# High weights over both halves of the activations in one 512-column matmul, halves added at read-out

## The chip, the cores and the metric

One core of a Trainium2 chip runs the whole layer. The time is device microseconds from start to end of one execution of that core's program; the median of several executions is compared.

## The reference

One layer of a hybrid backbone on 256 latent tokens and 256 context tokens of 4096 channels. Both are normed and modulated by an `adaLN` vector, then sent through one input projection of 13,312 columns, whose parts feed three mixers: a convolution module, a two-way gated linear recurrence and a neighbourhood attention that also reads the context. Each mixer's output is gated by a SiLU of its own part, all are concatenated, projected, added to the input and normed.

```python
hl = rmsnorm(xl, norm_g) * (1.0 + sc_l) + sh_l
hc = rmsnorm(xc, norm_g) * (1.0 + sc_c) + sh_c
a_val_l, a_glu_l, a_gate_l, r_x_l, r_gate_l, q_l, k_l, v_l, c_gate_l = split_proj(hl @ w_in)
... = split_proj(hc @ w_in)
...
mix_l = jnp.concatenate([ya_l * jax.nn.silu(a_gate_l), yb_l * jax.nn.silu(r_gate_l),
                         yc_l * jax.nn.silu(c_gate_l)], axis=-1)
xl_new = xl + g_l * (mix_l @ w_out)
```

All of it is in float32. The kernel makes each large float32 product out of three products of `float32r` operands: weights are split into a high part `hi` and a rest `lo`, activations likewise into part 0 and part 1, and it sums high x part 0, high x part 1 and low x part 0.

## The kernel before

The program is one long unrolled list in three phases. **Phase 1** (up to about 944 us of the trace) makes the modulation, the normed activations `LH` (latent) and `CH` (context), and those parts of the projection that both need (`r_x`, context keys, values) block by block over the contraction, with sums kept in pages `acc`. **Phase 2** (about 944 to 2004 us) makes the other parts of the projection for the latent tokens in chunks of 512 output columns over all 32 tiles of the contraction: values and gates of the convolution (`conv_in`), keys, queries and gates of four groups of four attention heads (`att_group`), and after these the gate of the recurrence, the pointwise product `w_pw` (8 tiles of contraction) and the gate of the convolution. **Phase 3** is the output projection (`gemm_tm`).

A chunk of phase 2 is one call of `gemm_cm` (L340): for each loaded pair of contraction tiles, four tiles of 128 output channels, and for each of these and each contraction tile `k` three matmuls of 256 moving columns (the 256 tokens): high weights on part 0, high weights on part 1, low weights on part 0, all into the same 256-column region of a bank. Each matmul has a weight load of its own. Two tiles of output channels share a bank of 512 columns, so a chunk takes two of the five banks of the tag "g" (L72). Phase 2 has 20 such chunks of 32 contraction tiles and 2 (`w_pw`) of 8.

`weights` (L327) loads 4 contraction tiles at a time as `raw` (1 MB on SP's queue, three buffers, shared with the loads of `w_ada` that `background` mixes in), ScalarE rounds two tiles to `hi` (L338), VectorE subtracts to get `lo` (L339); three buffers each. When a chunk ends its banks are read out by one instruction of 512 columns each, and the SiLU gates read the bank twice (L571, L572). Read-outs and the weight split stand under `hp()`, a high priority for the planner (`schedule_with_timeline_sim=True`), which fixes the order on each engine at build time. Convolutions, recurrences and the attention of heads go beside the products at lower priority; SBUF tiles come from one pool of `NPG` = 75 pages of 2 KB. GpSimd issues the attention's bias loads (L584).

In phase 1 the `r_x` chunks (`gemm_cm` with two moving operands) and the value chunks (`gemm_tm` with four stationary ones) each take four of the five banks "g"; they are emptied by `spill` (L499). Phase 3's `gemm_tm` uses matmuls of 512 columns, one weight load each.

Of the kernel before, what the change touches and what calls it, by code (L numbers as in the profile page):

```python
# [12 lines left out]
AF = mybir.ActivationFunctionType  # L13
# [11 lines left out]
    0, 1024, 2048, 3072, 4096, 5120, 7168, 9216, 11264)  # L25
# blocks of the contraction in the first phase, in tiles of 128
BLOCKS = [1, 2, 3, 3, 3, 4, 4, 4, 4, 4]
# from this block on, every second one's shift is summed on the vector engine
PAIRED = 8
# pages of 2 KB, buffers of weights as loaded and as split  # L30
NPG, NRAW, NHI = 75, 3, 3
# tiles of the contraction kept for the second half of the last chunk
HELD = 12
# urgency of what the tensor engine waits for
HP = 200000
# rates of the loads that go beside the products, by phase
ADA_A, ADA_B, CAP = 2.15, 1.2, 4.0
G1, G2, G3 = 0.4, 0.3, 0.4
# chunks of the last block that a recurrence follows; order of the second phase
REC1 = (1, 2, 4, 6, 8)  # L40
# [4 lines left out]
def tile_hybrid_layer(ctx: ExitStack, tc: tile.TileContext, x, c, cctx_tok, c_ctx, w_ada, b_ada,  # L45
# [13 lines left out]
    def background(weight):  # L59
        """emits queued units of loads between those of the products, at the set rate"""  # L60
        bg["credit"] = min(bg["credit"] + bg["rate"](weight), CAP)
        while bg["q"] and bg["credit"] >= 2.0:
            bg["credit"] -= 2.0
            bg["q"].pop(0)()
# [57 lines left out]

    # silu(c), silu(c_ctx) as channel columns, padded to 32 stationary columns
    scol = cp.tile([P, 64], F32, name="scol")
# [40 lines left out]
    def ada_units(k0, s, parts=(0, 1), on_vector=False):  # L165
# [92 lines left out]
    def rsqrt(y, v, t):  # L258
        """y = v ** -0.5, the table's root refined by a Newton step"""
        A.activation(y, v, AF.Sqrt)  # L260
        V.reciprocal(y, y)
        V.tensor_mul(t, y, y)
        V.tensor_mul(t, t, v)
        V.tensor_scalar(t, t, -0.5, 1.5, ALU.mult, ALU.add)
        V.tensor_mul(y, y, t)

# [1 line left out]
    ss = cp.tile([P, 4, 8], F32, name="ss")  # L268
# [56 lines left out]

# [1 line left out]
    def weights(view, ks, c0):  # L327
        """tiles of the weights, up to 4 loaded and 2 split at a time: [(tiles of the contraction, high, low)]"""
        for i in range(0, len(ks), 4):
# [12 lines left out]
    def gemm_cm(view, ks, c0, movs):  # L342
        """channel-major: out[n, t] for 4 tiles of n and each moving operand, 256 columns a region"""
        nb = 2 * len(movs)
# [14 lines left out]
        return banks  # L359

    def gemm_tm(view, ks, c0, stats, end=True):
        """token-major: out[t, n] for each stationary operand, 512 columns"""
        banks = [bank("g", "gtm") for _ in stats]
# [20 lines left out]
    def columns():  # L384
# [4 lines left out]
        V.tensor_scalar(hpw, col("b_pw", 0, 8), 0.5, None, ALU.mult)  # L389
        # 4 softplus(-lam), softplus(-lam) = (max(-lam, 0) + log1p(exp(-|lam|))), log1p(e) = 2 atanh(e / (2 + e))  # L390
        lm = col("lam", 0, 16)
# [21 lines left out]
    def ybs(n):  # L413
        """where the two directions' sum of head n lies: half a page of the inputs of a pair of heads"""
        return acc[("r", n // 4), n % 4 // 2 * 2][:, (n % 2) * T:(n % 2) * T + T]

    def recurrence(n):
# [22 lines left out]
        for d in range(2):  # L440
            xc, e, ti = rec[d]
            ci = cis[d]
            pr = bank("aux", "pr")
            nc.tensor.matmul(pr, gw[:, d, 0], xc, start=True, stop=True)
            pi = bank("aux", "pi")
            nc.tensor.matmul(pi, gw[:, d, 1], xc, start=True, stop=True)
            A.activation(ti, pi, AF.Tanh, bias=hbi[:, ci:ci + 1], scale=0.5)
            # 2 sigmoid(z) = exp(min(z, 0)) (1 + |tanh(z / 2)|)
            A.activation(e, pr, AF.Relu, bias=nbr[:, ci:ci + 1], scale=-1.0)
            A.activation(pr, pr, AF.Tanh, bias=hbr[:, ci:ci + 1], scale=0.5)  # L450
            prs.append(pr)
# [29 lines left out]

# [1 line left out]
    acc = {}  # L483
    side = [lambda n=n: recurrence(n) for n in range(8)]

    def aside(n=1):
        """emits the next pieces of work that need few products, among the chunks of those that need many"""
        for _ in range(n):
# [16 lines left out]
    while bi < len(BLOCKS):  # L505
        if bi < PAIRED:
            aq += ada_units(starts[bi], BLOCKS[bi])
        else:
            # the second block's shift is summed on the vector engine, spread among the other three parts
            pe = ada_units(starts[bi], BLOCKS[bi]) + [lambda bi=bi: done.add(bi)]  # L510
# [46 lines left out]

# [1 line left out]
    ALLK = list(range(KT))  # L559
# [6 lines left out]

    def silu2(b):
        """2 silu(b), a page"""
        t = page([P, 512], name="sil")
        with hp():  # L570
            A.activation(t, b, AF.Tanh, scale=0.5)  # L571
            V.scalar_tensor_tensor(t, t, 1.0, b, ALU.add, ALU.mult)  # L572
        return t

# [45 lines left out]

    # queries lie from right to left within a grid row, so that the bias rows are read with a stride of +1
    def att_group(g):
        kl, q, cg = [], [], []
        for b in gemm_cm(win, ALLK, C_K + 512 * g, [LH]):
            t = page([P, 2, T], name="kl")
            with hp():
                A.copy(t.rearrange("p a b -> p (a b)"), b)
            kl += [t[:, 0], t[:, 1]]
        aside()
        for b in gemm_cm(win, ALLK, C_Q + 512 * g, [LH]):  # L630
            t = page([P, 2, T], name="q")
            with hp():
                A.mul(t.rearrange("p a (r c) -> p (a r) c", c=64)[:, :, ::-1],
                      b.rearrange("p (r c) -> p r c", c=64), SCALE)
            q += [t[:, 0], t[:, 1]]
        aside()
        for b in gemm_cm(win, ALLK, C_CG + 512 * g, [LH]):
            t = silu2(b).rearrange("p (a b) -> p a b", a=2)
            cg += [t[:, 0], t[:, 1]]
# [6 lines left out]
    def conv_in(g):  # L646
        vals = []
        for b in gemm_cm(win, ALLK, C_VAL + 512 * g, [LH]):
            t = page([P, 512], name="val")
            with hp():  # L650
                A.mul(t, b, 0.5)
            vals.append(t)
        aside()
        for bi, b in enumerate(gemm_cm(win, ALLK, C_GLU + 512 * g, [LH])):
            t = page([P, 512], name="glu")
            with hp():
                A.activation(t, b, AF.Tanh, scale=0.5)
            for j in range(2):
# [59 lines left out]
    for g in range(2):  # L718
        for bi, b in enumerate(gemm_cm(win, ALLK, C_RG + 512 * g, [LH])):
            t = silu2(b)  # L720
            for j in range(2):
# [5 lines left out]
    for g in range(2):  # L727
        for bi, b in enumerate(gemm_cm(wpw, list(range(8)), 512 * g, [SH])):
            t = page([P, 512], name="pw")
            for j in range(2):  # L730
                n = 4 * g + 2 * bi + j
                with hp():
                    V.tensor_scalar(t[:, j * T:j * T + T], b[:, j * T:j * T + T], 0.25, hpw[:, n:n + 1],
                                    ALU.mult, ALU.add)
            PW.append(t)
    for g in range(2):
        for bi, b in enumerate(gemm_cm(win, ALLK, C_AG + 512 * g, [LH])):
            t = silu2(b)
            pw = PW[2 * g + bi]
# [3 lines left out]

# [1 line left out]
    korder = list(range(16, 32)) + list(range(8, 16)) + list(range(8))  # L745
# [3 lines left out]
    for oc in range(8):  # L749
# [27 lines left out]
        if oc < 7:  # L777
# [4 lines left out]
            continue  # L782
        # last chunk: the second token tile comes behind the first by HELD tiles of the contraction
        gate()
# [37 lines left out]
def _window():  # L822
    """neighbourhood mask by shape alone: rows are (query row parity, query column from the right),
    columns are key columns; a factor and an addend"""
    qc = 63 - np.arange(P) % 64
# [27 lines left out]
```

## Time and profile before

| | us |
|---|---|
| median of 3 executions | 2377.08 |
| lowest and highest | 2374.56, 2380.82 |
| span of the profiled execution | 2371.5 |
| TensorE busy with matmuls in it | 2315.1 (98%) |
| weight loads busy in it | 2034.4 (86%) |
| VectorE busy | 1580.3 (67%) |
| ScalarE busy | 945.7 (40%) |

The profiled execution is told by its span, from the first to the last instruction; the three timed executions lie 3 to 9 us above it. TensorE's two records of a product are read together: "PE" is the matmul, "PEld" the load of its stationary operand, which goes on while the matmul before it runs. A matmul's recorded duration overlaps the next one's, so its price is the distance from its start to the next start.

### The profile page before, as it was taken

The page shows a single profiled execution, that of the slowest core. Times are in us where ns is not written, and L with a number is a line of the kernel's source. Part 1 is how long each engine was busy: PE and PEld are TensorE (multiplying, and loading weights), DVE is VectorE, ACT ScalarE, POOL GpSimd, SP SyncE. Part 2 cuts the span into 40 slices and gives each one's busy share as a digit, 9 for nine tenths or more (in the row PEclk, how much of TensorE's full clock was granted, in tenths as well). Part 3 has the DMA queues.
Part 4 walks back from the last instruction along what each step waited for, and adds up shares of the span by engine and source line. Part 5 has one row for each costly group of instructions (what it writes and reads, how often), then busy time and mean ns, then how long its engine had stood idle before and what let it go on. Part 6 is the DMA issues. An engine that isn't in the chain of part 4 may idle for free.

```text
span 2371.5 us, 38433 instructions
## 1 busy us (share of the span) xinstructions
PE 2315.1 (98%) x16013; PEld 2034.4 (86%) x16013; DVE 1580.3 (67%) x2289; ACT 945.7 (40%) x1228; POOL 95.8 (4%) x150
## 2 busy tenths in 40 slices
PE   6899999999999999999999999999999999999997
PEld 4667777777788998999999899999999999888886
DVE  4465545445778779987879596955766666665555
ACT  5322212222223246886433343344444434434444
POOL 0000000000000001000000101101001001000000
PEclk9999999999999999999999999999999999999999
DMA  9888788877877544656776767767576678775664
GB/s 312 270 279 272 254 298 298 295 266 252 295 269 258 192 163 174 222 183 213 245 233 203 188 215 202 204 215 188 182 245 171 207 265 301 264 263 187 191 192 173
DMA packets 293461, 551.27 MB, mean 232 GB/s; under 512 B 10959, under 2 KB 52647, under 8 KB 293287
## 3 DMA queue, kind: packets, MB, share of 16 engines
q1 hardware_dynamic: 287856, 536.91, 66.1%
q0 software_dynamic: 4480, 11.54, 4.3%
q8 instruction: 125, 2.05, 0.3%
q10 hardware_dynamic: 951, 0.37, 0.1%
q14 instruction: 49, 0.40, 0.0%
HBM read 544.58 MB, written 4.19 MB: 231 GB/s over the span
## 4 chain that ended last, share of the span: by engine, by line
PE 83%; DMA 8%; DVE 4%; ACT 3%; issue 1%; SPq 0%; DVEq 0%; ACTq 0%
PE gcm L355 48%; PE gtm L371 9%; PE gtm L372 8%; PE gtm L370 8%; PE psa L217 5%; DMA raw<-in_w_ada_dram 4%; DMA raw<-in_w_in_dram 3%; DVE lo L339 2%; PE y L614 1%; ACT hi L338 1%; DMA xp<-in_ctx_dram 1%; DVE gacc L245 1%; PE pt L607 1%; PE sc L593 0%; PE sc L594 0%
## 5 line engine op out<-in xcount | busy, mean ns | idle before, releaser
L339 DVE TENSOR_TENSOR lo<-raw,hi 128x1024 fp32r<-128x1024 f32 (+1 forms) x630 | 747.4, 1189 | 556.8 <-ACT hi L338 552.9
L338 ACT CAST hi<-raw 128x1024 fp32r<-128x1024 f32 (+1 forms) x630 | 640.1, 1022 | 1171.9 <-PE gcm L355 492.8
L355 PE MATMUL gcm<-lh,hi 128*128 128x256 f32 x5632 | 1069.5, 285 | 2.9 <-ACT hi L338 2.8
L355 PEld LDWEIGHTS gcm<-lh,hi 128*128 128x128 f32 x5632 | 896.8, 192 | 18.3 <-issue 13.4
L355 PE MATMUL gcm<-lh,lo 128*128 128x256 f32 x2816 | 796.2, 285 | 4.2 <-DVE lo L339 4.0
L355 PEld LDWEIGHTS gcm<-lh,lo 128*128 128x128 f32 x2816 | 537.8, 192 | 11.6 <-DVE lo L339 5.8
L355 PE MATMUL gcm<-ch,hi 128*128 128x256 f32 x1536 | 326.6, 287 | 3.4 <-ACT hi L338 2.3
L355 PEld LDWEIGHTS gcm<-ch,hi 128*128 128x128 f32 x1536 | 259.0, 191 | 36.3 <-issue 27.8
L245 DVE SCALAR_TENSOR_TENSOR gacc<-raw,scol,gacc 128x512 f32<-128x512 f32 x248 | 185.8, 749 | 49.6 <-DMA raw<-in_w_ada_dram 47.1
L355 PE MATMUL gcm<-ch,lo 128*128 128x256 f32 x768 | 217.6, 286 | 0.0
L371 PE MATMUL gtm<-lo,mix 128*128 128x512 f32 x488 | 192.0, 393 | 0.1
L372 PE MATMUL gtm<-hi,mix 128*128 128x512 f32 x488 | 190.1, 390 | 0.0
L370 PE MATMUL gtm<-hi,mix 128*128 128x512 f32 x488 | 171.1, 390 | 0.0
L355 PEld LDWEIGHTS gcm<-ch,lo 128*128 128x128 f32 x768 | 146.5, 191 | 12.8 <-issue 9.0
L217 PE MATMUL psa<-raw,cpad 128*32 128x512 f32 (+3 forms) x1216 | 132.5, 521 | 7.9 <-DMA raw<-in_w_ada_dram 7.8
L499 DVE TENSOR_TENSOR acc<-acc,gcm 128x512 f32<-128x512 f32 x144 | 96.1, 682 | 37.7 <-PE gcm L355 37.1
L371 PEld LDWEIGHTS gtm<-lo,mix 128*128 128x128 f32 x488 | 91.6, 188 | 20.5 <-DVE lo L339 1.3
L370 PEld LDWEIGHTS gtm<-hi,mix 128*128 128x128 f32 x488 | 91.5, 188 | 19.2
L499 DVE TENSOR_TENSOR acc<-acc,gtm 128x512 f32<-128x512 f32 x144 | 94.3, 680 | 19.9 <-PE gtm L372 19.7
L372 PEld LDWEIGHTS gtm<-hi,mix 128*128 128x128 f32 x488 | 91.7, 188 | 18.4
L673 DVE SCALAR_TENSOR_TENSOR cv<-upad,cols,cv 128x256 f32<-128x256 f32 x240 | 105.6, 483 | 0.0
L371 PE MATMUL gtm<-lo,ch 128*128 128x512 f32 x256 | 102.2, 399 | 0.2 <-DVE lo L339 0.2
(218 smaller groups left out, 2107.9 us busy)
## 6 DMA issues: line engine op xcount, KB each, us to landing
raw<-in_w_in_dram SPq DMA_DIRECT2D x210, 1024.0 KB, 5.2
raw<-in_w_ada_dram SPq DMA_DIRECT2D x156, 1024.0 KB, 5.5
raw<-in_w_out_dram SPq DMA_DIRECT2D x61, 1024.0 KB, 5.5
raw<-in_w_ada_dram SPq DMA_DIRECT2D x48, 768.0 KB, 5.9
raw<-in_w_in_dram SPq DMA_DIRECT2D x30, 768.0 KB, 6.1
raw<-in_w_in_dram SPq DMA_DIRECT2D x10, 512.0 KB, 5.4
xp<-in_ctx_dram SPq DMA_DIRECT2D x16, 256.0 KB, 5.8
xp<-in_x_dram SPq DMA_DIRECT2D x16, 256.0 KB, 5.4
```

What stands on the lines that cost most here:

```text
L217: nc.tensor.matmul(st["ps"][32 * q:32 * q + 32, :W], cpad[k // 16][:, k % 16, :], raw[:, j, :], start=(k < 4), stop=(k >= KT - 4))
L245: V.scalar_tensor_tensor(st["a"], raw[:, j], s, st["a"], ALU.mult, ALU.add)
L338: A.copy(hi[:, :n], raw[:, o:o + n])
L339: V.tensor_sub(lo[:, :n], raw[:, o:o + n], hi[:, :n].bitcast(F32))
L355: nc.tensor.matmul(banks[r // 2][:, (r % 2) * T:(r % 2) * T + T], w[:, j, nt * P:(nt + 1) * P], movs[m][k][:, part], start=first, stop=las ...
L370: nc.tensor.matmul(banks[b], hh, wh[:, j], start=first, stop=False)
L371: nc.tensor.matmul(banks[b], hh, wl[:, j], start=False, stop=False)
L372: nc.tensor.matmul(banks[b], hl, wh[:, j], start=False, stop=last)
L499: V.tensor_add(acc[key, i], acc[key, i], b)
L607: nc.tensor.transpose(ps[:, kt * T + qt * P:kt * T + qt * P + P], Ps[qt][:, (2 * kp + kt) * P:(2 * kp + kt + 1) * P], ident)
L614: nc.tensor.matmul(ps[:, :T], acc[("v", h // 4), kt][:, i * P:(i + 1) * P], Ps[kt // 2][:, (kt % 2) * T:(kt % 2) * T + T], start=(kt == 0) ...
L673: V.scalar_tensor_tensor(o, upad[n][:, tap:tap + T], cw(tap, n), o, ALU.mult, ALU.add)
```

## The change

In phase 2 `gemm_cm` is replaced by `gemm_hl`: the high weights are loaded once and run over both parts of the activations as one matmul of 512 columns into a whole bank (left half the product with part 0, right half that with part 1); the low weights follow on part 0 into the left half. So two matmuls and two weight loads stand where three of each stood, and a chunk takes four banks. `joined` adds the halves at read-out: ScalarE copies the right half of each bank into a page, VectorE adds the left half to it. What follows (`tanh`, the reversed query copy, the SiLU product) then reads pages, at ordinary priority. The pool grows to 81 pages; the scratch for GpSimd's DMA descriptors is set to 4096. `gemm_cm` and `gemm_tm` stay in phases 1 and 3.

```diff
-NPG, NRAW, NHI = 75, 3, 3
+NPG, NRAW, NHI = 81, 3, 3
...
+    def gemm_hl(view, ks, c0, mov):
+
+        banks = [bank("g", "ghl") for _ in range(4)]
+        for kp, wh, wl in weights(view, ks, c0):
+            for nt in range(4):
+                for j, k in enumerate(kp):
+                    sl = slice(nt * P, (nt + 1) * P)
+                    nc.tensor.matmul(banks[nt], wh[:, j, sl], mov[k].rearrange("p a t -> p (a t)"),
+                                     start=k == ks[0], stop=False, skip_group_check=True)
+                    nc.tensor.matmul(banks[nt][:, :T], wl[:, j, sl], mov[k][:, 0],
+                                     start=False, stop=k == ks[-1], skip_group_check=True)
+            background(1)
+        return banks
+
+    def joined(banks, name, scale=None, bias=None):
+
+        for i in range(0, 4, 2):
+            u, t = page([P, 2, T], name="half"), page([P, 2, T], name=name)
+            with hp():
+                for j in range(2):
+                    b = banks[i + j]
+                    if bias is not None:
+                        A.activation(u[:, j], b[:, T:], AF.Identity, bias=bias[:, i + j:i + j + 1], scale=scale)
+                    elif scale is not None:
+                        A.mul(u[:, j], b[:, T:], scale)
+                    else:
+                        A.copy(u[:, j], b[:, T:])
+                    if scale is not None:
+                        V.scalar_tensor_tensor(t[:, j], b[:, :T], scale, u[:, j], ALU.mult, ALU.add)
+                    else:
+                        V.tensor_add(t[:, j], b[:, :T], u[:, j])
+            yield t, u
...
-    def silu2(b):
-        """2 silu(b), a page"""
-        t = page([P, 512], name="sil")
-        with hp():
-            A.activation(t, b, AF.Tanh, scale=0.5)
-            V.scalar_tensor_tensor(t, t, 1.0, b, ALU.add, ALU.mult)
-        return t
+    def silu2(zu):
+
+        z, u = zu
+        A.activation(u, z, AF.Tanh, scale=0.5)
+        V.scalar_tensor_tensor(u.rearrange("p a b -> p (a b)"), u.rearrange("p a b -> p (a b)"), 1.0,
+                               z.rearrange("p a b -> p (a b)"), ALU.add, ALU.mult)
+        return u.rearrange("p a b -> p (a b)")
...
-        for b in gemm_cm(win, ALLK, C_K + 512 * g, [LH]):
-            t = page([P, 2, T], name="kl")
-            with hp():
-                A.copy(t.rearrange("p a b -> p (a b)"), b)
+        for t, _ in joined(gemm_hl(win, ALLK, C_K + 512 * g, LH), "kl"):
...
-        for b in gemm_cm(win, ALLK, C_Q + 512 * g, [LH]):
-            t = page([P, 2, T], name="q")
-            with hp():
-                A.mul(t.rearrange("p a (r c) -> p (a r) c", c=64)[:, :, ::-1],
-                      b.rearrange("p (r c) -> p r c", c=64), SCALE)
+        for z, t in joined(gemm_hl(win, ALLK, C_Q + 512 * g, LH), "z", SCALE):
+            A.copy(t.rearrange("p a (r c) -> p (a r) c", c=64)[:, :, ::-1],
+                   z.rearrange("p a (r c) -> p (a r) c", c=64))
...
-        for b in gemm_cm(win, ALLK, C_VAL + 512 * g, [LH]):
-            t = page([P, 512], name="val")
-            with hp():
-                A.mul(t, b, 0.5)
-            vals.append(t)
+        for t, _ in joined(gemm_hl(win, ALLK, C_VAL + 512 * g, LH), "val", 0.5):
+            vals.append(t.rearrange("p a b -> p (a b)"))
...
-                with hp():
-                    V.tensor_scalar(t[:, j * T:j * T + T], b[:, j * T:j * T + T], 0.25, hpw[:, n:n + 1],
-                                    ALU.mult, ALU.add)
-            PW.append(t)
+        for t, _ in joined(gemm_hl(wpw, list(range(8)), 512 * g, SH), "pw", 0.25, hpw[:, 4 * g:4 * g + 4]):
+            PW.append(t.rearrange("p a b -> p (a b)"))
...
-    nc = _bacc.Bacc("TRN2", target_bir_lowering=False, num_devices=1)
+    nc = _bacc.Bacc("TRN2", target_bir_lowering=False, num_devices=1, dynamic_dma_scratch_size=4096)
```

The gates of attention, recurrence and convolution and the convolution's second input change in the same way as the queries: `gemm_hl`, `joined` into a page `z`, then `tanh` and product on pages.

## Rows read from the trace of the kernel before

**Rows 1.** The page's head: span, and TensorE's busy time and share

```profile
span 2371.5 us, 38433 instructions
PE 2315.1 (98%) x16013; PEld 2034.4 (86%) x16013; DVE 1580.3 (67%) x2289; ACT 945.7 (40%) x1228; POOL 95.8 (4%) x150
```

**Rows 2.** The chain that ended last: shares of the span by line

```profile
PE gcm L355 48%; PE gtm L371 9%; PE gtm L372 8%; PE gtm L370 8%; PE psa L217 5%; DMA raw<-in_w_ada_dram 4%; DMA raw<-in_w_in_dram 3%; DVE lo L339 2%; PE y L614 1%; ACT hi L338 1%; DMA xp<-in_ctx_dram 1%; DVE gacc L245 1%; PE pt L607 1%; PE sc L593 0%; PE sc L594 0%
```

**Rows 3.** Busy time by stretch; last: granted clock, DMA share, GB/s

```profile
944.00:2003.60 1059.60, 1047.32 (x8351) 1026.58 (x8351) 784.76 (x1122) 513.11 (x644) 79.66 (x113) 1.00 0.68 214
944.00:990.00 46.00, 45.78 (x356) 43.27 (x356) 42.87 (x55) 41.07 (x52) 2.72 (x5) 1.00 0.59 202
1140.00:1160.00 20.00, 20.00 (x169) 20.00 (x168) 18.63 (x31) 9.49 (x11) 0.00 (x0) 1.00 0.63 213
1320.00:1340.00 20.00, 15.66 (x116) 14.92 (x115) 11.71 (x18) 7.46 (x11) 3.30 (x4) 0.90 0.68 167
2280.00:2320.00 40.00, 40.00 (x178) 33.12 (x177) 20.88 (x21) 17.54 (x20) 0.00 (x0) 1.00 0.64 204
```

**Rows 4.** Groups by line and form: latent matmuls of `gemm_cm`, count first

```profile
L355 PE MATMUL gcm<-lh,hi 128*128 128x256 f32 x5632 | 1069.5, 285 | 2.9 <-ACT hi L338 2.8
L355 PE MATMUL gcm<-lh,lo 128*128 128x256 f32 x2816 | 796.2, 285 | 4.2 <-DVE lo L339 4.0
L355 PE MATMUL gcm<-sh,hi 128*128 128x256 f32 x128 | 23.1, 283 | 0.0
L355 PE MATMUL gcm<-sh,lo 128*128 128x256 f32 x64 | 18.1, 283 | 0.0
```

**Rows 5.** Timeline of matmuls in phase 2, 256 columns each; start first

```profile
1159.92 0.40 PE L355 MATMUL gcm<-lh,hi 128*128 128x256 f32 x2
1160.16 0.28 PE L355 MATMUL gcm<-lh,lo 128*128 128x256 f32 x1
1160.28 0.28 PE L355 MATMUL gcm<-lh,hi 128*128 128x256 f32 x1
```

**Rows 6.** The same in phase 3: first and last of ten, 512 columns

```profile
2195.12 0.39 PE L371 MATMUL gtm<-lo,mix 128*128 128x512 f32 x1
...
2197.16 0.39 PE L371 MATMUL gtm<-lo,mix 128*128 128x512 f32 x1
```

**Rows 7.** The same in phase 1, where 256 columns follow 512

```profile
812.66 0.39 PE L372 MATMUL gtm<-hi,lh 128*128 128x512 f32 x1
812.89 0.28 PE L355 MATMUL gcm<-ch,hi 128*128 128x256 f32 x1
...
813.00 0.28 PE L355 MATMUL gcm<-ch,hi 128*128 128x256 f32 x1
813.12 0.28 PE L355 MATMUL gcm<-ch,lo 128*128 128x256 f32 x1
```

**Rows 8.** Groups by line: read-outs, and the nearest of 256 columns

```profile
L627 ACT COPY kl<-gcm 128x512 f32<-128x512 f32 x8 | 4.4, 585 | 0.8 <-PE gcm L355 0.8
L685 ACT COPY lnt<-mu 128x256 f32<-128x256 f32 x1 | 0.4, 373 | 4.7 <-PE mu L682 4.7
L596 DVE TENSOR_TENSOR sc<-sc,B 128x256 f32<-128x256 f32 x32 | 13.4, 425 | 6.7 <-PE sc L594 6.7
```

**Rows 9.** Waits of weight loads for an emptied bank: total, times, longest

```profile
PEld gtm L371 <- DVE acc L499: 2.1, 3, 0.8
PEld gcm L355 <- DVE acc L499: 1.5, 2, 0.8
PEld gtm L370 <- DVE acc L499: 0.8, 1, 0.8
```

**Rows 10.** The chain around 1326 us, its longest piece

```profile
1325.78 9.78 DMA raw<-in_w_in_dram
```

**Rows 11.** GpSimd's bias loads: group by line, and time to landing

```profile
L584 POOL DMA_DIRECT2D B<-in_rpb_dram x32 | 21.1, 665 | 500.8 <-DVE sm L600 177.6 <-issue 165.4 <-DVE cv L673 94.7
B<-in_rpb_dram POOLq DMA_DIRECT2D x32, 96.0 KB, 6.2
```

More of the change, by code (lines that the diff above doesn't have):

```diff
@@ L623, in att_group @@
         kl, q, cg = [], [], []
-        for b in gemm_cm(win, ALLK, C_K + 512 * g, [LH]):
-            t = page([P, 2, T], name="kl")
-            with hp():
-                A.copy(t.rearrange("p a b -> p (a b)"), b)
+        for t, _ in joined(gemm_hl(win, ALLK, C_K + 512 * g, LH), "kl"):
             kl += [t[:, 0], t[:, 1]]
         aside()
-        for b in gemm_cm(win, ALLK, C_Q + 512 * g, [LH]):
-            t = page([P, 2, T], name="q")
-            with hp():
-                A.mul(t.rearrange("p a (r c) -> p (a r) c", c=64)[:, :, ::-1],
-                      b.rearrange("p (r c) -> p r c", c=64), SCALE)
+        for z, t in joined(gemm_hl(win, ALLK, C_Q + 512 * g, LH), "z", SCALE):
+            A.copy(t.rearrange("p a (r c) -> p (a r) c", c=64)[:, :, ::-1],
+                   z.rearrange("p a (r c) -> p (a r) c", c=64))
             q += [t[:, 0], t[:, 1]]
         aside()
-        for b in gemm_cm(win, ALLK, C_CG + 512 * g, [LH]):
-            t = silu2(b).rearrange("p (a b) -> p a b", a=2)
+        for zu in joined(gemm_hl(win, ALLK, C_CG + 512 * g, LH), "z"):
+            t = silu2(zu).rearrange("p (a b) -> p a b", a=2)
             cg += [t[:, 0], t[:, 1]]
@@ L647, in conv_in @@
         vals = []
-        for b in gemm_cm(win, ALLK, C_VAL + 512 * g, [LH]):
-            t = page([P, 512], name="val")
-            with hp():
-                A.mul(t, b, 0.5)
-            vals.append(t)
+        for t, _ in joined(gemm_hl(win, ALLK, C_VAL + 512 * g, LH), "val", 0.5):
+            vals.append(t.rearrange("p a b -> p (a b)"))
         aside()
-        for bi, b in enumerate(gemm_cm(win, ALLK, C_GLU + 512 * g, [LH])):
-            t = page([P, 512], name="glu")
-            with hp():
-                A.activation(t, b, AF.Tanh, scale=0.5)
+        for bi, (z, t) in enumerate(joined(gemm_hl(win, ALLK, C_GLU + 512 * g, LH), "z")):
+            A.activation(t, z, AF.Tanh, scale=0.5)
+            t = t.rearrange("p a b -> p (a b)")
             for j in range(2):
@@ L718, in tile_hybrid_layer @@
     for g in range(2):
-        for bi, b in enumerate(gemm_cm(win, ALLK, C_RG + 512 * g, [LH])):
-            t = silu2(b)
+        for bi, zu in enumerate(joined(gemm_hl(win, ALLK, C_RG + 512 * g, LH), "z")):
+            t = silu2(zu)
             for j in range(2):
@@ L727, in tile_hybrid_layer @@
     for g in range(2):
[L728 to L732, printed above, removed]
-                    V.tensor_scalar(t[:, j * T:j * T + T], b[:, j * T:j * T + T], 0.25, hpw[:, n:n + 1],
-                                    ALU.mult, ALU.add)
-            PW.append(t)
+        for t, _ in joined(gemm_hl(wpw, list(range(8)), 512 * g, SH), "pw", 0.25, hpw[:, 4 * g:4 * g + 4]):
+            PW.append(t.rearrange("p a b -> p (a b)"))
     for g in range(2):
-        for bi, b in enumerate(gemm_cm(win, ALLK, C_AG + 512 * g, [LH])):
-            t = silu2(b)
+        for bi, zu in enumerate(joined(gemm_hl(win, ALLK, C_AG + 512 * g, LH), "z")):
+            t = silu2(zu)
             pw = PW[2 * g + bi]
```

## The prediction

> **What bounds the kernel now.** I read the head of the page first: TensorE is busy for 2315.1 of 2371.5 us and its weight loads for 2034.4 [rows 1]. A matmul counted busy need not be at its best, so the next view is the chain that ended last: 48% of the span lies on the matmuls of L355, three shares of 8 to 9% on `gemm_tm`, and what is neither TensorE nor a load is 1 or 2% a line [rows 2]. L355 is the line the change takes out of phase 2. The stretches then say whether that stage has one limit all through: of 1059.6 us of phase 2 TensorE is idle for 12.3 (1059.6 less 1047.3), VectorE is at 74% and ScalarE at 48% [rows 3]. So a shorter matmul list is worth its whole length there, as long as the other engines and the loads keep up.
>
> What limits the matmuls themselves is seen where two kinds stand side by side. In phase 2's steady stream the weight loads are busy for 20.00 of 20.00 us; in phase 3, with 512 columns a matmul, for 33.12 of 40 [rows 3]. In phase 2 starts lie 0.12 us apart (three in 0.36 us) [rows 5]; in phase 3 nine steps take 2.04 us, 0.2267 us each [rows 6], which is less than two of 0.12. The third place decides between two readings. Where a 256-column matmul follows one of 512 in phase 1, the next start comes 0.11 us later and the one after that 0.12 later, 0.23 for the two [rows 7]. Half of 0.2267 is 0.1133. I read this so: columns cost 0.113 us per 256, and in a stream of 256-column matmuls the weight loads, which need 0.12 us each, set the pace; behind a long matmul the load is already done.
>
> **The change, part by part.** *Matmuls.* The groups count 5632 high and 2816 low matmuls on the latent activations; 512 and 256 of these belong to phase 1's two `r_x` chunks (32 tiles of contraction x 4 x 2 chunks x 2, or x 1), so 5120 and 2560 are in phase 2, and 128 and 64 more on `sh` [rows 4]. That is 2560 + 64 = 2624 triples. A triple costs 3 x 0.12 = 0.360 us. Its successor is one matmul of 512 and one of 256, each weight load behind the other: 0.2267 + 0.1133 = 0.340 us. That alternating stream isn't in the trace. Its bounds: if the 256 keeps its 0.12, 0.347 us, a saving of 0.0133 x 2624 = 35 us; by the row where 256 follows 512, 0.340 us and 0.020 x 2624 = 52 us; nothing at all if the 512 costs two of 0.12. I take 52 us, since the start behind the 512 is exactly the step that recurs in the new stream [rows 7].
>
> The Trainium skill, page "TensorE: Matmul & The Clock Gate", section "Back-to-back issue gap", gives a rule that speaks against the change: at full clock a lone matmul's gap is its columns over 2.4 GHz plus 2.5 ns. By it only 2.5 ns would go with each removed instruction, an estimate of 2624 x 2.5 ns = 6.6 us. The trace disagrees with it on the size of the steps (120 and 227 ns where it gives 109 and 216), and the same section says of streams with weight loads that both operations set the spacing.
>
> *Read-out.* A chunk was emptied by two ScalarE instructions of 512 columns (0.585 us, the key copy) or by a pair of reads per bank. Now it takes four ScalarE reads of 256 columns, nearest row 0.373 us, and four VectorE sums, nearest row 0.425 us [rows 8]; the `tanh` and the reversed copy are still there, on pages. Over 22 chunks VectorE gains 88 x 0.425 = 37 us less eight replaced operations of `w_pw`, some 33 us net; ScalarE gains 88 x 0.373 = 33 us, plus eight reversed copies (4.7 us), less the 20 reads of keys, queries and values that fall away (20 x 0.585 = 12 us), some 26 us. Phase 2's VectorE goes from 784.8 of 1060 us to about 818 of 1010, 81%; ScalarE to 53%. Both lie beside the matmuls. The cover is thin in one place: from 944 to 990 us VectorE is at 93% and ScalarE at 89% [rows 3], with the recurrences. The recurrences and convolutions beside it are needed only later and can slip, so I take 1 us, with 0 to 5 as bounds (what two to four chunks add, 1.7 us of VectorE each).
>
> *Banks.* A chunk takes four of five banks, so the second output tile of the next chunk waits until the first bank is emptied. Its last matmul ends three blocks before the chunk's end (a block is two contraction tiles on one output tile, 2 x 0.34 = 0.68 us) and the bank is wanted one block after it: 2.7 us for a chain of 0.373 + 0.425 us, and the same for each bank behind it. Queued behind the waiting weight load on TensorE is the whole next chunk. The trace has this pattern: phase 1's 20 `r_x` and 40 value chunks take four of five banks, and their weight loads waited 2.1 + 1.5 + 0.8 = 4.4 us in all for VectorE's emptying [rows 9], 0.07 us a chunk. For 22 chunks that is 1.6 us, which I take. The other end is the whole chain with a weight split of 1.2 us ahead of it, 2.0 us x 22 = 44 us. Not below nothing: a wait for banks is not among the old read-out's costs.
>
> *Feed.* Loads, splits and rounding are unchanged in number and have to come 5% faster. Phase 2 moved 214 GB/s at a DMA share of 0.68 [rows 3], so 225 is wanted on average. The one stage where the feed already ends last is by the attention of the first heads: a piece of 9.78 us waits for `raw` [rows 10], in that stretch of 20 us TensorE is busy for 15.66 and its granted clock is 0.90, so part of it ran at the lower of the two levels, 1.2 GHz, after idling [rows 3]. That is some 4 us of idling and 2 of clock. I take 4 us of loss for the phase; the bounds are a gain of 6 (that stall falls away in a new order) and a loss of 20 (three more like it, one for each group of heads).
>
> *Pages and descriptors, costed at nothing.* `joined` holds two more pages at a time for each half chunk, and the pool has six more. For a read-out to wait for a page, work of low priority would have to hold some four more than it does by the list. The smaller descriptor scratch touches GpSimd's loads only: 0.665 us to issue, 6.2 us to land [rows 11]. If the second of a head's two bias loads had to wait for the first to land, that would be 6.2 us x 16 heads = 99 us at most, on an engine that is busy for 80 of 1060 us [rows 3]; the heads lie more than 6.2 us apart in most of the phase, so it is kept as a tail. The Trainium skill, page "SBUF — State Buffer", section "SBUF size: 192, 224, or 256?", says that the 16 KiB set aside by default are the ring of these descriptors; no run here shows how full it gets.
>
> *Sum:* -52 + 1 + 1.6 + 4 = -45 us, a span of 2326. The three executions' median lies 5.6 us above the profiled span, so 2332 us. With every term at its good end: -52 - 6 = -58, 2319 us. At the bad end short of the rivals: -35 + 5 + 4 + 20 = -6, 2371 us.
>
> **The rivals.**
> 1. *The weight load still sets the short matmul's price*, 0.347 us a pair: -35 + 6.6 = -28, 2349 us. For it: the steady 0.12. Against: the 0.11 behind a 512.
> 2. *The feed becomes the bound around the attention*: the 20 us above are lost, -52 + 20 + 3 = -29 to, with rival 1, -12: 2348 to 2365 us. For it: 9.78 us on the chain. Against: 12.3 us idle in all today.
> 3. *The change doesn't do what it says*: columns alone cost, and 512 of them cost two of 0.12. Then nothing is saved, the 6.6 us of small costs stay: 2384 us, within 0.3%. Against it: 2.04 us for nine steps. By the rule on the gap above it would be 2377.
> 4. *Slower: the bank wait.* If VectorE's in-order queue brings the sums of each bank 5.7 us late, 3 us past the cover of 2.7, TensorE stands still for 3 us at each of 22 chunks: 66 us, -52 + 66 + 5 = +19, 2396 us. It makes the kernel slower by more than 7 us from a delay of some 5.2 us a bank (47 + 7 = 54 us, 2.5 us past the cover at each chunk). For it: VectorE at 93% in two stretches, 18.63 of 20 and 42.87 of 46 [rows 3]. Against: 4.4 us in 60 chunks of the same pattern.
>
> **How the numbers follow.** Forecast 0.60, rival 1 0.12, rival 2 0.10, rival 3 0.05, rival 4 0.07; 0.06 stay for orders that I can't work out (pages, descriptors), half of them within 0.3%, half slower. A measurement of this kernel tells about 0.3%, 7 us, from no change. Faster by more: 0.60 + 0.12 + 0.10 = 0.82; within: 0.05 + 0.03 = 0.08; slower: 0.07 + 0.03 = 0.10. The range goes from the good end, 2318, to the bad end short of the rivals that save nothing, 2371, and leaves out 0.18.
>
> **What would show it.** In the changed kernel's timeline a 512 start is followed after 0.227 us by a 256 and after 0.113 more by the next 512; weight loads are no longer busy all the time in phase 2; phase 2 lasts about 1014 us where it lasted 1060, phases 1 and 3 as long as before. Weight loads waiting for a sum of `joined` come to under 3 us. I am wrong if pairs take 0.347 or 0.36 us, if weight loads wait for VectorE's sums by tens of us, or if TensorE's idle time in phase 2 grows well beyond 20 us.

## The result, and the profile after

The changed kernel takes 2398.06 us (median of 4 runs, 2396.9 to 2401.6), the kernel before 2376.4 us in the same comparison (2374.56 to 2380.82, 4 runs): a ratio of 1.0089 [1.0073, 1.0104]. Forecast were 2332 us and a range up to 2371, so both the sign and the range were missed. The profiled execution has a span of 2395.5 us at a mean granted clock of 0.986; before it was 2371.5.

The page of the changed kernel: its head, the chain's shares by line, and the groups of the new matmuls (busy, mean ns of one, idle time before them and what ended it).

```profile
span 2395.5 us, 33326 instructions
PE 2302.7 (96%) x13389; PEld 1897.0 (79%) x13389; DVE 1602.9 (67%) x2369; ACT 968.2 (40%) x1304; POOL 90.3 (4%) x150
...
PE ghl L368 22%; PE gcm L355 14%; PE ghl L370 11%; PE gtm L404 10%; PE gtm L405 10%; PE gtm L403 9%; PE psa L217 4%; DMA raw<-in_w_ada_dram 3%; DMA raw<-in_w_in_dram 3%; DVE lo L339 1%; PE y L647 1%; ACT hi L338 1%; PE pt L640 1%; DMA xp<-in_x_dram 0%; PE sc L626 0%
...
L368 PE MATMUL ghl<-lh,hi 128*128 128x512 f32 x2560 | 879.9, 398 | 25.3 <-DVE kl L391 20.6
L370 PE MATMUL ghl<-lh,lo 128*128 128x256 f32 x2560 | 665.1, 284 | 6.2 <-DVE lo L339 6.0
```

The 2624 matmuls are gone (16013 to 13389), and on the chain the two lines of `gemm_hl` (22 and 11%) stand for most of L355's 48% [rows 1, 2]. But TensorE's busy time falls by no more than 12.4 us, and the span grows by 24. Idle time in front of L368 is 25.3 us, and 20.6 of it is put down to one line: L391, VectorE's sum of the two halves of a key bank, in `joined`.

Where the span grew is read by phases, with the same two marks in each trace: the last `spill` of phase 1 and the first matmul of the output projection. Phase 2 by these marks, from the windows view of the kernel before, then of the changed one (start:end, length, busy time and count of PE, PEld, DVE, ACT, POOL; granted clock, DMA share, GB/s):

```profile
941.00:2003.60 1062.60, 1050.32 (x8369) 1028.86 (x8368) 787.00 (x1126) 516.11 (x649) 80.19 (x114) 1.00 0.68 214
```

```profile
951.30:2028.00 1076.70, 1033.07 (x5736) 887.41 (x5736) 804.29 (x1195) 529.36 (x710) 74.62 (x114) 0.98 0.67 211
```

Phase 2 is 14.1 us longer instead of 46 shorter. TensorE's busy time in it fell by 17.3 us, its idle time rose from 12.3 to 43.6. Phase 3 is the same (367.9 and 367.5 us). Phase 1 ended 10.3 us later; that end lay anywhere from 941.0 to 951.3 us in the nine profiled executions of all kernels that kept the low pass, 950.4 in one with the old matmuls, so one execution of each can't put those 10 us down to the change.

The idle time is in few places. Windows of 20 us of the changed kernel, first a dense one (as that from 1140 us in [rows 3]), then the four that hold 34.2 of the 43.6 us:

```profile
1160.00:1180.00 20.00, 20.00 (x117) 17.50 (x116) 18.86 (x31) 7.39 (x7) 0.00 (x0) 1.00 0.77 261
```

```profile
1340.00:1360.00 20.00, 10.68 (x46) 7.94 (x44) 12.53 (x26) 5.72 (x13) 4.91 (x6) 0.86 0.50 117
1360.00:1380.00 20.00, 17.35 (x75) 14.30 (x76) 12.72 (x27) 6.58 (x11) 1.99 (x2) 0.79 0.29 50
1520.00:1540.00 20.00, 12.32 (x50) 9.40 (x49) 13.04 (x33) 4.53 (x12) 3.31 (x4) 0.83 0.50 116
1700.00:1720.00 20.00, 5.46 (x17) 4.72 (x18) 14.85 (x41) 8.68 (x21) 0.00 (x0) 0.57 0.00 0
```

In the dense window weight loads are no longer busy all the time (17.50 of 20, 20.00 before), as was forecast. In the last one TensorE does 5.46 us of work, no byte is loaded, and the granted clock is 0.57. The waits view names what ends these stops (total, times, longest):

```profile
PE ghl L368 <- DVE kl L391: 20.6, 3, 16.6
PE pt L640 <- DVE pr L634: 10.2, 6, 4.3
```

```profile
PEld ghl L368 <- DVE kl L391: 5.1, 2, 2.6
PEld gcm L355 <- DVE acc L532: 1.5, 2, 0.8
```

The second fence holds the answer to [rows 9]: phase 1's waits of the same kind (1.5 us here and 0.6 for `gtm`) are as short as before. Three stops belong to key sums, one of them 16.6 us long; another 10.2 us, in six pieces, are waits of the attention's transposes (L640), while TensorE had little else that it could do. What VectorE and ScalarE did in the longest stop, from the timeline (start, length, operation; [idle before <- releaser]), VectorE's last operations, then ScalarE's, then TensorE's first ones after it:

```profile
1712.74 0.42 DVE L725 SCALAR_TENSOR_TENSOR cv<-sq,cv 128x256 f32<-128x256 f32 x1
1713.09 0.98 DVE L728 TENSOR_TENSOR sh<-cv,sh 128x256 fp32r<-128x256 f32 x2
1713.98 1.41 DVE L391 TENSOR_TENSOR kl<-ghl,half 128x256 f32<-128x256 f32 x4
```

```profile
1702.97 1.28 ACT L723 ACT_TABLE_LOAD   x1 [4.09 <-DVE cv L722]
...
1713.20 0.41 ACT L727 CAST sh<-cv 128x256 fp32r<-128x256 f32 x1 [0.32 <-DVE cv L725]
1713.51 1.19 ACT L387 COPY half<-ghl 128x256 f32<-128x256 f32 x4
```

```profile
1714.54 0.77 PE L368 MATMUL ghl<-lh,hi 128*128 128x512 f32 x1 [16.64 <-DVE kl L391]
1715.11 0.41 PE L370 MATMUL ghl<-lh,lo 128*128 128x256 f32 x1
1715.32 0.63 PE L368 MATMUL ghl<-lh,hi 128*128 128x512 f32 x1
1715.75 0.41 PE L370 MATMUL ghl<-lh,lo 128*128 128x256 f32 x1
```

ScalarE stood idle for 4.09 us inside the stop, with the key banks written and no matmul under way. The copies of the key halves have high priority, yet all four of them run in one block after the last `sh` cast of the convolution's layer norm. At the two other stops the sum comes right behind the last `mix` product of a head (the other pair starts at 1536.45 and 1536.79 us):

```profile
1366.27 0.87 DVE L598 TENSOR_TENSOR mix<-half,mix 128x256 fp32r<-128x256 f32 x1 [0.47 <-ACT mix L597]
1367.07 1.07 DVE L391 TENSOR_TENSOR kl<-ghl,half 128x256 f32<-128x256 f32 x3
```

So the key read-outs stand behind work of low priority that the list has ahead of them. What the two have in common is the pool: `half` and `kl` each ask for a page, and so did the work ahead. That is the theory that the runs below test.

What a pair costs is read in the dense window, where the groups of the timeline run on (x2 is one matmul joined with the next):

```profile
1159.86 0.40 PE L368 MATMUL ghl<-lh,hi 128*128 128x512 f32 x1
1160.09 0.40 PE L370 MATMUL ghl<-lh,lo 128*128 128x256 f32 x2
1160.33 0.40 PE L368 MATMUL ghl<-lh,hi 128*128 128x512 f32 x1
```

From 512 to 256 it is 0.23 us; from there to the second 256 of the x2 and on to the next 512, 0.24 for two. Over all of phase 2 (start to start, leaving out steps of 0.25 us and more) a 512-column matmul with a 256 behind it takes 233 ns, a 256 with a 512 behind it 117 ns, and the mean over both kinds is 175.2 ns, so 0.350 us a pair, where 0.340 was forecast.

### The profile page after: what moved, and what is told of

The parts are those of the page before. It is cut to its first block, busy times and chain, and to the rows that moved or that the text cites. A ratio compares the mean times of both kernels' runs of the same rounds, so it can differ in the third digit from the quotient of the medians.

```text
span 2395.5 us, 33326 instructions
## 1 busy us (share of the span) xinstructions
PE 2302.7 (96%) x13389; PEld 1897.0 (79%) x13389; DVE 1602.9 (67%) x2369; ACT 968.2 (40%) x1304; POOL 90.3 (4%) x150
## 4 chain that ended last, share of the span: by engine, by line
PE 86%; DMA 6%; DVE 4%; ACT 3%; issue 1%; SPq 0%; POOL 0%; DVEq 0%; ACTq 0%; POOLq 0%
PE ghl L368 22%; PE gcm L355 14%; PE ghl L370 11%; PE gtm L404 10%; PE gtm L405 10%; PE gtm L403 9%; PE psa L217 4%; DMA raw<-in_w_ada_dram 3%; DMA raw<-in_w_in_dram 3%; DVE lo L339 1%; PE y L647 1%; ACT hi L338 1%; PE pt L640 1%; DMA xp<-in_x_dram 0%; PE sc L626 0%
## 5 line engine op out<-in xcount | busy, mean ns | idle before, releaser
L368 PE MATMUL ghl<-lh,hi 128*128 128x512 f32 x2560 | 879.9, 398 | 25.3 <-DVE kl L391 20.6
L370 PE MATMUL ghl<-lh,lo 128*128 128x256 f32 x2560 | 665.1, 284 | 6.2 <-DVE lo L339 6.0
L368 PEld LDWEIGHTS ghl<-lh,hi 128*128 128x128 f32 x2560 | 472.8, 189 | 118.8 <-issue 20.9
L370 PEld LDWEIGHTS ghl<-lh,lo 128*128 128x128 f32 x2560 | 484.6, 189 | 37.3 <-DVE lo L339 12.3
L355 PE MATMUL gcm<-ch,hi 128*128 128x256 f32 x1536 | 328.6, 288 | 2.6 <-ACT hi L338 2.6
L355 PEld LDWEIGHTS gcm<-ch,hi 128*128 128x128 f32 x1536 | 260.4, 192 | 33.9 <-issue 25.3
L355 PE MATMUL gcm<-ch,lo 128*128 128x256 f32 x768 | 216.7, 286 | 1.1 <-DVE lo L339 1.1
L355 PEld LDWEIGHTS gcm<-ch,lo 128*128 128x128 f32 x768 | 146.0, 191 | 16.0 <-issue 11.8
L355 PE MATMUL gcm<-lh,hi 128*128 128x256 f32 x512 | 136.1, 288 | 0.0
L355 PEld LDWEIGHTS gcm<-lh,hi 128*128 128x128 f32 x512 | 99.0, 194 | 10.1 <-issue 9.8
```

The source lines that it names most:

```text
L355: nc.tensor.matmul(banks[r // 2][:, (r % 2) * T:(r % 2) * T + T], w[:, j, nt * P:(nt + 1) * P], movs[m][k][:, part], start=first, stop=las ...
L368: nc.tensor.matmul(banks[nt], wh[:, j, sl], mov[k].rearrange("p a t -> p (a t)"), start=k == ks[0], stop=False, skip_group_check=True)
L370: nc.tensor.matmul(banks[nt][:, :T], wl[:, j, sl], mov[k][:, 0], start=False, stop=k == ks[-1], skip_group_check=True)
```

## The experiments

The theory after the first comparison: four of five banks are held until the key read-out, and the key read-out waits for a page of the shared pool behind work ahead of it in the list; the pair is worth less than forecast. The rivals: too few pages; four banks and read-outs in halves at their own price; VectorE's queue; a joined matmul that saves nothing. "Own" below is a tag of six pages for the key read-outs alone.

**e1, key read-outs in pages of their own.**

```diff
-NPG, NRAW, NHI = 81, 3, 3
+NPG, NRAW, NHI = 75, 3, 3
+    def own(shape, name):
+        uid[0] += 1
+        return pg.tile(shape, F32, name=f"{name}_{uid[0]}", tag="own", bufs=6)
...
-            u, t = page([P, 2, T], name="half"), page([P, 2, T], name=name)
+            mk = own if name == "kl" else page
+            u, t = mk([P, 2, T], name="half"), mk([P, 2, T], name=name)
```

> The changed kernel, but the pages that the key chunk's read-out fills (kl and its half) come from six pages of their own; the common pool goes from 81 to 75, so there are 81 in all as before. Theory (order of pages): in the changed kernel the key read-out of a group stands behind the attention of the group before and behind the convolution's norm, since the common pool hands out pages in program order; with four of five banks held, TensorE stops. With own pages these stops (16.6 us after the norm, some 12 and 8 us after two groups) go: 2398 less 35 to 45, so 2353 to 2363 us, and weight loads and matmuls wait for kl sums for under 3 us. Rival (queues): the sums are late because VectorE and ScalarE are full, whoever owns the page: 2394 to 2402 us. Rival (too few pages): the common pool is now smaller, 2400 us or more.

Measured: 2352.79 us (2351.24 to 2358.56), a ratio to the kernel before of 0.9896 [0.9881, 0.9911]; 45 us less than the changed kernel, by where six pages of 81 come from. Its phase 2, its key sums around the layer norm of the changed kernel's long stop, and what is left of the two waits:

```profile
948.20:1989.40 1041.20, 1027.82 (x5745) 885.26 (x5744) 807.89 (x1203) 536.50 (x721) 78.19 (x113) 1.00 0.70 218
```

```profile
1664.62 0.75 DVE L396 TENSOR_TENSOR kl<-ghl,half 128x256 f32<-128x256 f32 x2
1669.62 0.42 DVE L396 TENSOR_TENSOR kl<-ghl,half 128x256 f32<-128x256 f32 x1
1671.09 0.42 DVE L396 TENSOR_TENSOR kl<-ghl,half 128x256 f32<-128x256 f32 x1
```

```profile
PE ghl L372 <- DVE kl L396: 1.0, 1, 1.0
PE pt L645 <- DVE pr L639: 3.1, 2, 2.4
```

The sums come one by one, ahead of that layer norm (its last `sh` is at 1720 us here), not four in a block behind it. TensorE's idle time in phase 2 is 13.4 us, 30.2 less; its busy time is 5.3 us less (less work at the lower clock level behind a stop: the granted clock of phase 2 is 1.00, where it was 0.98); together the 35.5 us by which phase 2 is shorter. This version beats both kernels. (Its profiled execution was the longest of the four, 2358.56 us.)

**e4, the changed kernel with 75 pages** instead of 81 and the default descriptor memory.

```diff
-NPG, NRAW, NHI = 81, 3, 3
+NPG, NRAW, NHI = 75, 3, 3
...
-    nc = _bacc.Bacc("TRN2", target_bir_lowering=False, num_devices=1, dynamic_dma_scratch_size=4096)
+    nc = _bacc.Bacc("TRN2", target_bir_lowering=False, num_devices=1)
```

> The changed kernel with the pool of 75 pages and the default scratch of the kernel before. Theory (order of pages, not their number): the key read-outs stand in the same places, TensorE's stops stay, 2386 to 2402 us; towards the lower end if phase 1's 9 us come from the pool. Rival (too few pages make the read-outs late): six pages fewer make it much worse, 2410 us or more.

Measured: 2402.63 us (2401.04 to 2403.91), 1.0101 [1.0086, 1.0116]. The stops are those of the changed kernel:

```profile
PE ghl L368 <- DVE kl L391: 20.2, 3, 16.7
```

So between 75 and 81 it isn't the number of pages: six fewer move the time by 4.6 us and the long stop by 0.1. A much larger pool was not run. What e1 altered was whose pages the read-outs draw on.

**e3, the kernel before with 81 pages** and the descriptor memory at 4096.

```diff
-NPG, NRAW, NHI = 75, 3, 3
+NPG, NRAW, NHI = 81, 3, 3
...
-    nc = _bacc.Bacc("TRN2", target_bir_lowering=False, num_devices=1)
+    nc = _bacc.Bacc("TRN2", target_bir_lowering=False, num_devices=1, dynamic_dma_scratch_size=4096)
```

> The kernel before with only the pool of 81 pages and the descriptor scratch of 4096. In the changed kernel's trace phase 1, whose code is the same, ends about 9 us later than before. Theory (pool and scratch alter phase 1's planned order): 2383 to 2388 us. Rival (it is chance or comes from elsewhere): 2373 to 2380 us. No theory expects the waits of phase 2 from it.

Measured: 2379.65 us (2377.0 to 2384.46, 10 runs), 1.0015 [1.0002, 1.0027], some 3 us. Neither the pool nor the smaller descriptor memory is the cause of the changed kernel's 22 us.

**e2, the old three matmuls, but each output tile in a bank of its own**, so that a chunk holds four of five banks without any joined matmul; the read-outs become two of 256 columns where there was one of 512.

```diff
+    def gemm_4(view, ks, c0, mov):
+        banks = [bank("g", "g4") for _ in range(4)]
...
+                    for qi, (w, part) in enumerate(((wh, 0), (wh, 1), (wl, 0))):
+                        nc.tensor.matmul(banks[nt][:, :T], w[:, j, nt * P:(nt + 1) * P], mov[k][:, part],
...
-                A.copy(t.rearrange("p a b -> p (a b)"), b)
+                for j in range(2):
+                    A.copy(t[:, j], b[j])
```

> The kernel before with its three matmuls of 256 columns, but each tile of output channels in a bank of its own, so that a chunk of phase 2 takes four banks of five, left half of each; read-outs of 256 columns, no sum of halves, 75 pages. Theory (banks): the demand for banks alone makes TensorE wait for the key read-outs behind attention and norm, so 35 to 45 us more than the kernel before, 2411 to 2421 us. Rival (the sum at read-out, its operations and pages, is what costs): within 6 us of the kernel before, 2370 to 2382 us.

Measured: 2428.88 us (2426.35 to 2429.67), 1.021 [1.0195, 1.0225], 52 us slower than the kernel before and more than was expected. Phase 2, and the waits:

```profile
943.50:2058.90 1115.40, 1061.93 (x8371) 1034.58 (x8370) 789.65 (x1141) 519.61 (x688) 76.64 (x114) 0.98 0.66 205
```

```profile
PE g L367 <- ACT kl L641: 18.6, 3, 16.1
PE g L367 <- DVE lo L339: 13.1, 7, 8.3
```

The same three stops for keys, the longest 16.1 us, and here ScalarE's copy ends them: the key read-out has no VectorE sum in this kernel. So VectorE's queue is not what makes it late. Another 13.1 us are waits for split weights, 8.3 of them in one piece.

**e7, the kernel before with own pages for its keys**, and **e8, e2 with own pages for its keys** (both with six own pages beside 75 and the descriptor memory at 4096).

```diff
-            t = page([P, 2, T], name="kl")
+            t = own([P, 2, T], "kl")
```

> The kernel before with the key read-outs in pages of their own (six under a tag of their own beside the 75, the descriptor memory at 4096 bytes as in the changed kernel), its three 256-column matmuls and two banks a chunk as they were. It shows whether run e1's gain over the kernel before comes from the joined matmul or from the key pages alone. Theory (with two of five banks held, TensorE went on in the other three while the key read-out waited for a page; phase 2 of the kernel before has only 12 us of idle TensorE): no change, 2370 to 2384 us. Rival (the late pages cost the kernel before as well, so that e1's 24 us are theirs and the joined matmul is worth nothing): 2352 to 2364 us.

> The kernel of run e2 (three 256-column matmuls as before, but each output tile in a bank of its own, so four of five banks a chunk) with the key read-outs in pages of their own, six beside the 75. Theory (e2's 52 us over the kernel before are the stops of TensorE while four banks wait for the keys' pages): most of them go, idle TensorE in phase 2 falls from 53 us to 12 to 25 us, 2380 to 2402 us. Rival (four banks and the read-outs in halves cost by themselves, whatever the keys' pages): 2415 to 2432 us.

Measured: e7 2382.35 us (2379.03 to 2386.17, 10 runs), 1.0024 [1.0012, 1.0036]; e8 2387.29 us (2383.08 to 2397.63, 8 runs), 1.0040 [1.0025, 1.0055]. Phase 2 of e7, then of e8 (whose profiled execution was its longest, 2397.63):

```profile
947.60:2011.60 1064.00, 1050.22 (x8371) 1028.89 (x8370) 787.68 (x1126) 515.85 (x650) 77.65 (x114) 1.00 0.69 214
```

```profile
950.10:2027.10 1077.00, 1052.85 (x8366) 1030.55 (x8366) 788.38 (x1141) 517.87 (x687) 76.37 (x114) 0.99 0.69 212
```

With two banks a chunk the pages are worth nothing, 5 us lost if anything: e1's gain is not the pages' alone. With four banks they are worth 42 us. What is left of e8's idle time, 24.2 us where e7 has 13.8, holds no stop for keys; the longest sums of waits in it are those of TensorE for split weights (10.7 us) and rounded ones (8.0 us). The runs make a table of medians in us:

| phase 2's matmuls and banks | keys in shared pages | keys in own pages |
|---|---|---|
| three of 256, two banks a chunk | 2377 (before, all its runs) | 2382 (e7) |
| three of 256, four banks | 2429 (e2) | 2387 (e8) |
| one of 512 and one of 256, four banks | 2398 (changed) | 2353 (e1) |

Down the columns: four banks cost 52 us with shared pages and 5 with own ones; the joined matmul gains 31 and 34. Across: own pages gain nothing with two banks, 42 and 45 with four. In the first two rows the kernels on the right have six pages more than their neighbours on the left and the smaller descriptor memory; e3 puts that at some 3 us.

**e5, e1 with the highs of a pair of contraction tiles first, then its lows.**

```diff
             for nt in range(4):
                 for j, k in enumerate(kp):
...
+            for nt in range(4):
+                for j, k in enumerate(kp):
+                    sl = slice(nt * P, (nt + 1) * P)
                     nc.tensor.matmul(banks[nt][:, :T], wl[:, j, sl], mov[k][:, 0],
```

> This is the kernel of run e1 (the changed kernel, its key sums in pages of their own) with one thing altered: within each pair of contraction tiles of a head group all eight high 512-column matmuls are issued first and then all eight low 256-column ones, in place of high, low, high, low. In e1's and the changed kernel's traces a 512-column step that follows a 256-column one takes 233 ns and the 256-column step 118 ns, a pair 0.351 us where phase 3's 512-column stream takes 0.227 us a step. Theory (the price is that of the change of width, what follows a 256-column step pays it): in runs of eight the 512-column steps fall from 233 to about 228 to 230 ns, the pair to 0.345 to 0.348 us, 2624 pairs give 8 to 15 us: 2338 to 2345 us. Rival (the price belongs to the 512-column matmul of these operands, whatever stands before it): no change, 2350 to 2358 us, and the steps stay at 233 and 118 ns.

Measured: 2364.05 us (2361.63 to 2366.56), 0.9945 [0.9926, 0.9965]: 11 us slower than e1, so both expected times are missed. The timeline shows the new order:

```profile
1161.03 1.11 PE L377 MATMUL ghl<-lh,lo 128*128 128x256 f32 x8
1161.99 2.00 PE L372 MATMUL ghl<-lh,hi 128*128 128x512 f32 x8
1163.83 1.11 PE L377 MATMUL ghl<-lh,lo 128*128 128x256 f32 x8
```

Eight lows take 0.96 us, 0.120 each, and eight highs 1.84, 0.230 each. By place in the run of eight, the mean steps of the 512-column ones are 233, 234, 229, 232, 230, 227, 227 and 227 ns: those behind the change of width pay, and by the sixth the pace of phase 3 is reached. The 256-column ones, 117 ns when they alternate, take 120 in a run. What the highs gain the lows lose: over whole blocks the median is 0.349 us a pair, 0.350 in e1. The loss goes with the feed, as far as it was followed: the waits of TensorE for rounded weights (L342) rose from 0.9 us, once, to 7.5 us, six times:

```profile
PE ghl L372 <- ACT hi L342: 7.5, 6, 4.7
```

TensorE's idle time in phase 2 went from 13.4 to 20.5 us, 7 of the 11. Why weights arrive later in this order was not followed further.

**e6, e1 without the low pass**, to see the 512-column matmul alone.

```diff
-                                     start=k == ks[0], stop=False, skip_group_check=True)
-                    nc.tensor.matmul(banks[nt][:, :T], wl[:, j, sl], mov[k][:, 0],
-                                     start=False, stop=k == ks[-1], skip_group_check=True)
+                                     start=k == ks[0], stop=k == ks[-1], skip_group_check=True)
```

> The kernel of run e1 without the low pass of the second phase's joined multiplication: each pair is its 512-column matmul alone. Left out: the product of the low weights with the first part of the activations, in all four multiplications that the second phase makes with joined columns, so its output is that of the high weights alone. This is for the price of the 512-column step alone. Theory (233 ns is paid because a 256-column step went before): the dense steps of the second phase are 227 ns, as in phase 3, and the phase, if VectorE and ScalarE kept up, would be 2624 x 0.118 + 2624 x 0.006 = 325 us shorter; since VectorE alone is busy for over 800 us of it, the phase comes out at 850 to 950 us and only the steps between two waits are of use. Rival (the price belongs to these operands or their banks): 231 to 234 ns in the dense steps.

Measured: 2297.06 us in one run. The phase is set by the feed, 980 us long rather than the 850 to 950 expected; only its dense groups are of use, of which this is the longest:

```profile
1798.82 23.87 PE L372 MATMUL ghl<-lh,hi 128*128 128x512 f32 x104 [1.21 <-ACT hi L342]
```

103 steps and a last matmul of some 0.39 us: 0.228 us a step; the mean of all its steps under 0.24 us is 0.228 as well, at a granted clock of 1.00 in this stretch. With the same operands and the same banks, the 512-column matmul costs what it costs in phase 3 once no 256-column one stands beside it.

## Why the prediction was wrong

*What bounds the kernel, and the marks of the change*: right. Phase 2 is TensorE's; the 2624 matmuls fell away; the weight loads are no longer busy all through; phases 1 and 3 have their lengths, apart from what single executions scatter in phase 1.

*Matmuls, -52 us*: the term that was mis-sized, by some 20 us. The two steps read from [rows 6] and [rows 7] were added as if the new stream paid each of them in turn. The 256 behind the 512 did come near its 0.113 (0.117), but the 512 behind the 256 costs 0.233, not 0.2267. Against the kernel before (0.360 us a triple in its steady runs; 0.362 from the mean of its steps, 120.6 ns) the pair saves 0.010 to 0.0113 us, times 2624 27 to 30 us; the table has 31 and 34. So the price of rival 1 was nearly right, 0.350 for its 0.347, and its reason was not: the short matmul got cheaper and the long one dearer. The trace of before showed this, where phase 3 begins behind a 256-column stream:

```profile
2003.49 0.28 PE L355 MATMUL gcm<-lh,lo 128*128 128x256 f32 x1
2003.61 0.40 PE L370 MATMUL gtm<-hi,mix 128*128 128x512 f32 x1
2003.84 0.40 PE L371 MATMUL gtm<-lo,mix 128*128 128x512 f32 x1
...
2004.77 0.39 PE L372 MATMUL gtm<-hi,mix 128*128 128x512 f32 x1
```

From the first 512 to the sixth (2004.77) five steps take 1.16 us, 0.232 each, where [rows 6] has 0.2267. The prediction read only the change from 512 to 256, and a stream that alternates has both. Of the rule of the Trainium skill that the prediction set against this term ("TensorE: Matmul & The Clock Gate", section "Back-to-back issue gap"), by which 6.6 us would go, the runs agree on the direction of the error only: 27 to 34 us went.

*Banks, +1.6 us*: the step that failed. Four banks cost 52 us here (before to e2), more than the upper bound of 44. The cover of 2.7 us and the chain of 0.8 us were not the point: what was missing is that a read-out may be unable to start. With own pages four banks cost 5 us (e7 to e8), not far from what the row on phase 1 promised. That row [rows 9] was a bad likeness: after a first block `spill` adds into sums that hold their pages already, while `joined` asks for new ones.

*Pages, costed at nothing*: the reason for it. It asked whether there are enough pages, and six more or fewer change nothing (e4 stops just as long). By the runs what counts is whose pages they are: a read-out of high priority is late as long as its page comes from the pool that it shares with work of low priority ahead of it in the list. The kernel before has the same lateness without the price. Its key copies of the last group stand right behind the last `sh` cast, as in the changed kernel; in e7 they come some 40 us earlier (1684.95 and 1690.72 us), before that layer norm's casts:

```profile
1726.41 0.71 ACT L703 CAST sh<-cv 128x256 fp32r<-128x256 f32 x2
1727.02 1.07 ACT L627 COPY kl<-gcm 128x512 f32<-128x512 f32 x2
```

But its keys held two of five banks, TensorE had the other three for the next chunk, and e7 gains nothing. The lateness was thus in the trace before the change.

*Feed, +4, and the other engines, +1*: not what made the kernel slower. With the stops gone e1's phase 2 has 13.4 us of idle TensorE, 12.3 before, at 218 GB/s. It is 21.4 us shorter than before, though, not 27 to 30: steps of its chunks that are over 15 ns longer than usual lose 32.8 us in all, 22.6 before. That execution was e1's longest, and what held each step up was not followed. e5 shows that there isn't much to spare: an order of the same work lost more at the feed than it gained in steps.

*The sum in measured parts*: +52 for four banks (42 of them go with own pages for the keys) and -31 for the matmuls make +21 for the change. By way of e2 the two parts add up to the measured difference whatever the cause. What speaks for the split is the other column of the table, where the matmuls come to -34 by other kernels.

*Rival 4*, with 0.07, had the place (a wait for banks at read-out), the sign, and with 2396 us almost the time. The time agrees by chance: it was to be 3 us at each of 22 chunks from VectorE's queue; it was three stops, one of them 16.6 us, and e2 stops as long with no sum on VectorE. Of the signs of being wrong that the prediction named, three came: a pair near 0.347 us, TensorE's idle time in phase 2 well beyond 20 us (43.6), and waits for VectorE's sums by tens of us, though the trace has these as waits of the matmuls (20.6 us) more than of their weight loads (5.1).

That pages are given out in the order of the list is a reading of the traces (what runs just ahead of the late read-outs) and of e1, e4 and e8 together; the hand-out itself is in no trace.

## What to carry over

When a change makes a chunk hold more of the banks, ask of its read-outs not only how long they take but what each must have before it may start: a page from a pool shared with slack work hands that work's lateness to the engine that waits for the bank. A small tag of its own for such read-outs cost at most 5 us where it wasn't needed (e7), and here it turned +0.9% into -1.0%. A price for an alternating stream needs both changes of width from the trace, not one.

## What was not expected of the hardware

A 512-column matmul is dearer for some five steps after a 256-column one (233, 234, 229, 232, 230 ns against 227 in the long run), and the 256 behind a 512 cheaper (117 against 120). Arranged one by one or eight by eight, the pair came to 0.350 and 0.349 us, against 0.347 for the two at their own pace (0.227 + 0.120). The section of the Trainium skill named above says that in a stream of weight loads and matmuls both set the spacing. The runs fit that (a 256 takes 120 ns in its own stream, 117 behind a 512) but don't separate the two. For such a stream the section gives about 131 ns at 512 columns; here phase 3 takes 227 ns a step.

After the stop of 16.64 us the matmuls ran at the lower of the two levels: the timeline has 0.43 us for a 512 and 0.21 for a 256 up to 1719.80, and the window's granted clock is 0.57. Behind the stop of 2.19 us, at 1367.53 us, the first steps were short, and those from 1368.41 to 1371.61 us were 0.43 and 0.21 us again. Behind the one of 1.74 us, at 1537.27 us, the next two steps were 0.33 and 0.12 us.
